# Three plain feed-forward chunks instead of four, later down units, other places for the down inputs

## The chip, the cores and the metric

The kernel runs on one core of a Trainium2 chip. The metric is device time in microseconds (us) for one launch, the median of several runs. The core has a matmul engine (TensorE, here PE), a vector engine (VectorE, DVE), an activation engine (ScalarE, ACT), a general engine (GpSimd, POOL) and a queue that issues most transfers (SyncE, SP). They run side by side and wait for each other through semaphores.

## The reference

Two layers of an encoder, 512 tokens of 1024 channels, float32. Each has three branches (two attentions and a pooling) that are merged, and then a gated feed-forward part with 2 x 2816 inner channels:

```
hf = rms_norm(x, ffn_norm_g[l])
u = depthwise_conv(hf @ ffn_w_up[l], ffn_conv_w[l], ffn_conv_b[l])   # width 3 over tokens
u_gate, u_val = u[..., :D_FF], u[..., D_FF:]
x = x + (jax.nn.silu(u_gate) * u_val) @ ffn_w_down[l]
```

Only the schedule of this last part changes.

## The kernel before, in words

**Numbers.** Every float32 operand is split into a high and a low half, and each product is three matmuls: high by high, low by high, high by low (`mm3`). Activations lie with channels on the 128 partitions and the 512 tokens along the row.

**Chunks.** The 2816 inner channels are 22 chunks of 128. A chunk has a gate part (part 0) and a value part (part 1). It can be made in two ways.

- A *plain* chunk (`plain`) multiplies each part with all eight blocks of 128 input channels: 8 x 3 matmuls of 128x512 per part, 48 in all, into one PSUM bank per part.
- A chunk of *products* (`product`) takes gate and value rows, odd and even input blocks, and first and second half of the tokens as a 2x2 by 2x2 block product and makes it with seven products instead of eight. They are named 11, 12, 1, 22, 2, 4, 3 (`FORMS`, in this order). Each has four steps of three matmuls of 128x256, so 12, and the chunk 84. Products 11, 12 and 4 read the normalized input (tiles HH, HL); 1, 2, 22 and 3 read sums of its blocks (tiles `tf`), which `build_forms` makes on DVE and ACT once per layer, while the plain chunks run on PE.

**What else a chunk needs.** The weights come from HBM by SP into `raw` tiles. A plain piece is split by ACT (`wh`) and by DVE, POOL or an accumulating transfer (`wl`). For a chunk of products four blocks of 128x512 arrive. Blocks 11, 12, 22 are split into `fh` and `fl`, where the low half is finished by a transfer that POOL issues (`by_transfer`); for products 1, 2, 4, 3 DVE sums blocks, ACT takes the high half and DVE the low one (`w_form`). Weight units are made up to six units ahead of their use (`wnext`, LAF). Behind the products DVE adds the banks to saved pieces (`sx`, by ACT), scales by the norm, adds the two neighbours of the convolution, multiplies gate by value and makes the low half; ACT does the middle tap, the SiLU and the high half.

**Down units.** A down unit (`down`) is three matmuls of 128x512: one chunk of the group before, into one block m of 128 output channels. The units of a group g go over its 8 blocks m, and over its chunks i inside; after the last i DVE adds the bank (`ps_mi`, `ps_S` in turn) to the residual XM. So no unit of a group can come before the group's chunk that it reads is finished and split.

**The order.** The chunks form groups (`SIZES`). `_ffn` writes PE's order out: all plain chunks of group 0, then for each chunk of products the seven products, and after products 22, 2, 4 and 3 (`SPOTS`, four *places* per chunk) some down units of the group before, dealt evenly over the group's places. Two chunks' worth (`KEEP` 2 output blocks) of the last-but-one group's units and all of the last group's come behind the last product. `_stream` derives the order of the weight loads from the same list. The orders of DVE, ACT, POOL and SP come out of a model of the engines' times inside the kernel (`Clock`), which decides only order, while the program is written.

**Where the halves wait.** A chunk's high and low half wait for the down units of the next group. The first ones of a group take fixed places (six pairs in four wide tiles `act`, `PLACE`), the others two slots each (`ah`, `al`) of a pool of 47 slots of 128x512 that all temporary tiles share (`keep_act`).

In the last layer the last block m is made in two token halves (`half`, `out_half`), so that its first half can be stored earlier; of each unit but the last three the second half follows at once.

Of the kernel before, what the change touches and what calls it, by code (L numbers as in the profile page):

```python
# [21 lines left out]
KC = D // P  # L22
# [4 lines left out]
FC = D_FF // P  # L27
# [14 lines left out]
PRE_A = 16  # L42
PRE_B = 8
LA, LAP, LAF = 3, 4, 6
SIZES = (4, 5, 5, 5, 3)
PLACE = ((0, 1, 2, 3), (4, 5), (0, 1, 2, 3), (4, 5), (0, 1, 2))
KEEP = 2
FORMS = ("11", "12", "1", "22", "2", "4", "3")
SPOTS = ("22", "2", "4", "3")
END = object()  # L50
RSQRT_BITS = 1597463007.0
SLACK = 35
# [57 lines left out]
def _groups():  # L110
    e = np.cumsum(SIZES)
    return [(int(b - n), int(b)) for n, b in zip(SIZES, e)]


def _ffn():

    toks, late = [], []
    for g, (c0, c1) in enumerate(_groups()):  # L120
        dealt = len(late) - (KEEP * SIZES[g - 1] if g == len(SIZES) - 1 else 0)
        for n, c in enumerate(range(c0, c1)):
            if g == 0:
                toks += [("u", c, 0), ("u", c, 1)]
                continue
            now = late[:dealt * (n + 1) // (c1 - c0) - dealt * n // (c1 - c0)]
            late = late[len(now):]
            for f in FORMS:
                toks.append(("f", c, f))
                if f in SPOTS:  # L130
                    k = SPOTS.index(f)
                    toks += now[len(now) * k // len(SPOTS):len(now) * (k + 1) // len(SPOTS)]
        late += [("d", g, m, i) for m in range(KC) for i in range(c1 - c0)]
    return toks + late


def _layer_units():

    r = _widths()
    for tok in _ffn():  # L140
        if tok[0] == "u":
            r += [("u", T), ("p", T), ("next",)]
        elif tok[0] == "f":
            r.append(tok)
        elif (tok[2] * SIZES[tok[1]] + tok[3]) % 4 == 0:
            r.append(("u" if tok[1] < len(SIZES) - 1 else "p", T))
    return r


def _stream():  # L150
# [4 lines left out]
    for kind, *u in _layer_units() * L:  # L155
        if kind == "next":
            plain = (plain + 1) % (2 * SIZES[0])
            if plain >= 2 * SIZES[0] - 8 or not plain:
# [179 lines left out]
def trunk(ctx: ExitStack, tc: tile.TileContext, x, w, prm, gb, cst, out):  # L338
# [344 lines left out]
    def layer(l, sq, xsrc):  # L683
# [331 lines left out]
        def gates(br, okey, odst, mode):  # L1015
# [48 lines left out]
            for k, m in _order(br):  # L1064
# [5 lines left out]
                while more:  # L1070
                    n = tick - first
                    if extra and (tick % 2 == 0 if when == "q" else k == "g" and n in ((2, 6) if when == "n" else (3,))):
                        if next(extra, END) is END:
                            extra = None
                        yield
                    tick += 1
                    more = next(work, END) is not END
                    yield
# [570 lines left out]
        def keep_act(c):  # L1649
            g = next(i for i, (c0, c1) in enumerate(groups) if c0 <= c < c1)  # L1650
            i = c - groups[g][0]
            if i < len(PLACE[g]):
                n = 2 * PLACE[g][i]
                return places[n], places[n + 1]
# [156 lines left out]
        for kind, *tok in _ffn():  # L1811
            {"u": plain, "f": product, "d": down}[kind](*tok)
# [64 lines left out]
def _pack_weights(i):  # L1877
    res = []
    for l in range(L):
# [34 lines left out]
        for kind, *tok in _ffn():  # L1914
            if kind == "u":
                c, part = tok
                o = D_FF * part + c * P
                res += _cut(_blocks(up[:, o:o + P], KC))
            elif kind == "f" and tok[1] == FORMS[0]:
                for o in (0, D_FF):  # L1920
                    b = _blocks(up[:, o + tok[0] * P:o + tok[0] * P + P], KC).reshape(P, KC // 2, 2, P)
                    res += [b[:, :, k].reshape(P, T) for k in range(2)]
            elif kind == "d":
                g, m, k = tok
                c0, c1 = _groups()[g]
                if (m * (c1 - c0) + k) % 4 == 0:
                    at = [divmod(m * (c1 - c0) + k + n, c1 - c0) for n in range(4)]
                    res.append(np.concatenate([dn[(c0 + k_) * P:(c0 + k_ + 1) * P, m_ * P:m_ * P + P]
                                               for m_, k_ in at], axis=1))
# [82 lines left out]
```

## Time and profile before

| | |
|---|---|
| median of 3 runs | 1545.17 us (1543.88 to 1545.56) |
| the profiled execution's own time | 1543.25 us |
| its span, first to last instruction | 1541.4 us |
| feed-forward stage of layer 0 | 425.27 to 771.49 us |
| plain chunks of layer 0 | 425.27 to 469.04 us |
| chunks of products of layer 0 | 469.04 to 748.37 us |
| feed-forward stage of layer 1 | from 1191.7 us to the end |

The span is what the trace shows; the execution's own time has 1.85 us more around it. Times in rows of the trace are microseconds from the start of the span. A row of a group or instruction names the line, the engine, the operation and output<-inputs without buffer numbers. A matmul's row shows longer than the distance to the next one, since matmuls overlap; PE's pace is read from start to start, or from a long stretch divided by its count. Lines are those of the kernel before; the changed kernel's are 14 higher behind the edit.

### The profile page before, as it was taken

The numbers are of one execution on the slowest core, as the hardware profiler recorded it, in microseconds if no ns is written. First come the engines' busy times: TensorE is split into PE (matmuls) and PEld (weight loads), VectorE is DVE, ScalarE is ACT, GpSimd is POOL, SyncE is SP. The second block draws the span as 40 slices with busy tenths as digits, with TensorE's granted clock in tenths as the row PEclk, the third lists the DMA queues.
The fourth block names the chain that finished last, engine by engine and source line by source line (L and its number), as shares of the span: only waits on it lengthen the run. The fifth ranks groups of instructions, "written<-read, shape, count | busy, mean of one in ns | idle before, by whom it ended". The sixth has DMA issues, their size and how long they took to land.

```text
span 1541.4 us, 24574 instructions
## 1 busy us (share of the span) xinstructions
PE 1535.9 (100%) x8337; PEld 1343.0 (87%) x8337; DVE 1157.5 (75%) x1955; ACT 1079.5 (70%) x2018; POOL 765.6 (50%) x829
## 2 busy tenths in 40 slices
PE   9999999999999999999999999999999999999999
PEld 8888888888889999999898888888888899999997
DVE  6767886776688888888746588768666888888885
ACT  6567875877677877777554587758766677777772
POOL 3874886753452323232488648776535522222222
PEclk9999999999999999999999999999999999999999
DMA  7432354658978878877554423547599788787863
GB/s 239 113 117 83 88 125 141 161 130 205 235 170 195 181 184 187 190 175 160 139 148 126 118 74 88 125 144 174 117 217 217 193 183 191 178 188 190 179 140 109
DMA packets 140381, 243.36 MB, mean 158 GB/s; under 512 B 31072, under 2 KB 53600, under 8 KB 140256
## 3 DMA queue, kind: packets, MB, share of 16 engines
q1 hardware_dynamic: 91872, 162.93, 34.2%
q0 software_dynamic: 43488, 78.66, 29.7%
q8 instruction: 65, 1.06, 0.3%
q10 hardware_dynamic: 4896, 0.21, 0.2%
q14 instruction: 60, 0.49, 0.1%
HBM read 149.41 MB, written 13.63 MB: 106 GB/s over the span
## 4 chain that ended last, share of the span: by engine, by line
PE 95%; DMA 2%; POOL 1%; issue 1%; DVE 1%; ACT 0%; SPq 0%; POOLq 0%; ACTq 0%; DVEq 0%
PE ps_acc L526 42%; PE ps_AV L526 17%; PE ps_ST L526 16%; PE ps_S L526 10%; PE ps_mi L526 9%; DMA XM<-x 1%; DMA qb<-nm 1%; DMA raw<-w 0%; POOL win L306 0%; DMA tf<-dl 0%; POOL tabg L306 0%; POOL tabm L306 0%; POOL fac L306 0%; POOL wl L306 0%; POOL ssc L306 0%
## 5 line engine op out<-in xcount | busy, mean ns | idle before, releaser
L438 POOL DMA_DIRECT2D wl<-raw x194 | 174.9, 908 | 407.2 <-ACT wl L299 183.8
L299 ACT ACTIVATE wh<-raw 128x512 fp32r<-128x512 f32 (+2 forms) x449 | 265.0, 605 | 61.4 <-DMA raw<-w 17.6
L306 POOL TENSOR_TENSOR wl<-raw,wh 128x512 fp32r<-128x512 f32 (+2 forms) x164 | 204.9, 1258 | 147.1 <-ACT wh L299 141.5
L438 POOL DMA_DIRECT2D fl<-raw x108 | 94.2, 872 | 167.5 <-ACT fl L299 67.3
L526 PE MATMUL ps_acc<-HH,wh 128*128 128x512 f32 x400 | 156.7, 392 | 0.0
L526 PE MATMUL ps_acc<-HH,wl 128*128 128x512 f32 x400 | 156.4, 391 | 0.0
L526 PE MATMUL ps_acc<-HL,wh 128*128 128x512 f32 x400 | 156.4, 391 | 0.0
L310 DVE SCALAR_TENSOR_TENSOR a<-u,prm,a 128x511 f32<-128x511 f32 x176 | 134.4, 766 | 19.0 <-ACT a L299 18.4
L299 ACT ACTIVATE wl<-wh 128x512 fp32r<-128x512 f32 (+1 forms) x194 | 121.9, 628 | 6.2
L314 DVE TENSOR_REDUCE nm<-ps_S 128x1 fp32r<-128x512 f32 x128 | 87.7, 686 | 44.2 <-PE ps_S L526 43.6
L299 ACT ACTIVATE a<-u,prm 128x512 f32<-128x512 f32 x88 | 71.2, 812 | 56.2 <-DVE u L306 56.0
L526 PE MATMUL ps_acc<-tf,wh 128*128 128x256 f32 x576 | 106.2, 282 | 0.0
L526 PEld LDWEIGHTS ps_acc<-tf,wh 128*128 128x128 f32 x576 | 94.3, 191 | 6.0
L526 PEld LDWEIGHTS ps_acc<-HH,wl 128*128 128x128 f32 x400 | 75.1, 188 | 16.3
L526 PEld LDWEIGHTS ps_acc<-HL,wh 128*128 128x128 f32 x400 | 75.2, 188 | 15.4
L526 PEld LDWEIGHTS ps_acc<-HH,wh 128*128 128x128 f32 x400 | 75.3, 188 | 15.1 <-issue 0.4
L526 PE MATMUL ps_acc<-tf,wl 128*128 128x256 f32 x288 | 81.5, 283 | 0.0
L306 DVE TENSOR_TENSOR wl<-raw,wh 128x512 fp32r<-128x512 f32 (+1 forms) x92 | 64.3, 700 | 18.6 <-ACT wh L299 18.2
L526 PE MATMUL ps_AV<-HH,wl 128*128 128x256 f32 (+1 forms) x240 | 78.2, 326 | 0.0
L526 PE MATMUL ps_AV<-HH,wh 128*128 128x256 f32 (+1 forms) x240 | 78.1, 326 | 0.0
L526 PE MATMUL ps_AV<-HL,wh 128*128 128x256 f32 (+1 forms) x240 | 78.1, 326 | 0.0
L306 DVE TENSOR_TENSOR pl<-ps_ST,ph 128x512 fp32r<-128x512 f32 x86 | 58.3, 682 | 17.8 <-ACT ph L299 14.3
(427 smaller groups left out, 5028.2 us busy)
## 6 DMA issues: line engine op xcount, KB each, us to landing
raw<-w SPq DMA_DIRECT2D x153, 512.0 KB, 4.0
wl<-raw POOLq DMA_DIRECT2D x190, 256.0 KB, 4.2
raw<-w SPq DMA_DIRECT2D x151, 256.0 KB, 3.8
fl<-raw POOLq DMA_DIRECT2D x108, 256.0 KB, 5.0
raw<-w SPq DMA_DIRECT2D x13, 384.0 KB, 3.1
XM<-x SPq DMA_DIRECT2D x16, 256.0 KB, 4.4
dtq<-tr SPq DMA_DIRECT2D x16, 192.0 KB, 1.9
dtk<-tr SPq DMA_DIRECT2D x16, 192.0 KB, 3.0
```

The source lines that it names most:

```text
L299: return self.eng.activation(out, in_, func, **k)
L306: return self.eng.tensor_tensor(out, *a)
L310: return self.eng.scalar_tensor_tensor(out, *a)
L314: return self.eng.tensor_reduce(out, in_, *a, **k)
L438: nc.gpsimd.dma_start(f(lo), r, accum_op=ALU.add)
L526: PE.matmul(o, lhsT=lhsT, rhs=rhs, start=start, stop=stop, skip_group_check=again)
```

## The change

Group 0 has three plain chunks instead of four and the last group four chunks of products instead of three, so that 19 chunks of a layer are made by products instead of 18. The places are counted through from the first chunk of products. A new table `SKIP` lets the down units of groups 1, 2 and 3 (dealt while groups 2, 3 and 4 are made) begin one place later; the first place of such a group still takes units of the group before. The fixed places are given out as 0 to 2 and 3 to 5 by turns.

```
-SIZES = (4, 5, 5, 5, 3)
-PLACE = ((0, 1, 2, 3), (4, 5), (0, 1, 2, 3), (4, 5), (0, 1, 2))
+SIZES = (3, 5, 5, 5, 4)
+PLACE = ((0, 1, 2), (3, 4, 5), (0, 1, 2), (3, 4, 5), (0, 1, 2))
 KEEP = 2
 FORMS = ("11", "12", "1", "22", "2", "4", "3")
 SPOTS = ("22", "2", "4", "3")
+SKIP = (0, 0, 1, 1, 1)
...
+def _dealt():
+
+    starts = [len(SPOTS) * (c0 - SIZES[0]) + n for (c0, _), n in zip(_groups(), SKIP)]
+    at = [0] * (len(SPOTS) * (FC - SIZES[0]))
+    for g in range(1, len(SIZES)):
+        a, n = starts[g], starts[g + 1 if g + 1 < len(SIZES) else g] - starts[g]
+        units = KC * SIZES[g - 1]
+        if not n:
+            n = len(at) - a
+            units -= KEEP * SIZES[g - 1]
+        for s in range(n):
+            at[a + s] = units * (s + 1) // n - units * s // n
+    return at
...
-    toks, late = [], []
+    toks, late, dealt = [], [], iter(_dealt())
     for g, (c0, c1) in enumerate(_groups()):
-        dealt = len(late) - (KEEP * SIZES[g - 1] if g == len(SIZES) - 1 else 0)
         for n, c in enumerate(range(c0, c1)):
             if g == 0:
                 toks += [("u", c, 0), ("u", c, 1)]
                 continue
-            now = late[:dealt * (n + 1) // (c1 - c0) - dealt * n // (c1 - c0)]
-            late = late[len(now):]
             for f in FORMS:
                 toks.append(("f", c, f))
                 if f in SPOTS:
-                    k = SPOTS.index(f)
-                    toks += now[len(now) * k // len(SPOTS):len(now) * (k + 1) // len(SPOTS)]
+                    k = next(dealt)
+                    toks += late[:k]
+                    late = late[k:]
         late += [("d", g, m, i) for m in range(KC) for i in range(c1 - c0)]
     return toks + late
```

The new deal puts 24 units on 21 places (1 each, 2 at three of them), then 2 on each of the other 55. Before it was 32 on 20 places, 40 on 20, 40 on 20 and 30 on 12.

PE behind the third plain chunk of layer 0, before: the last matmuls of its value part (bank ps_AV) and the first of the fourth plain chunk (`wh`, `wl` are split weights).

```order
L526 MATMUL ps_AV_4988<-HH,wh_4942 128x512
L526 MATMUL ps_AV_4988<-HL,wh_4942 128x512
L526 MATMUL ps_AV_4988<-HH,wl_4943 128x512
L526 MATMUL ps_acc_5047<-HH,wh_4946 128x512
L526 MATMUL ps_acc_5047<-HL,wh_4946 128x512
L526 MATMUL ps_acc_5047<-HH,wl_4947 128x512
```

The same place after: product 11 of the first chunk of products follows (`fh`, `fl` are the halves of block 11).

```order
L540 MATMUL ps_AV_4998<-HH,wh_4899 128x512
L540 MATMUL ps_AV_4998<-HL,wh_4899 128x512
L540 MATMUL ps_AV_4998<-HH,wl_4900 128x512
L540 MATMUL ps_acc_5052<-HH,fh_4903 128x256
L540 MATMUL ps_acc_5052<-HL,fh_4903 128x256
L540 MATMUL ps_acc_5052<-HH,fl_4904 128x256
```

The two parts of the fourth plain chunk (48 matmuls of 128x512) are gone from here, and the products stand in their place.

PE at the first place of group 4 in layer 0, before: the end of product 22 (bank ps_ST), the first two down units of group 3 (bank ps_mi, halves in the fixed places `act`) and product 2.

```order
L526 MATMUL ps_ST_8144<-tf_4766,fh_8010 128x256 x2
L526 MATMUL ps_ST_8144<-tf_4766,fl_8011 128x256
L526 MATMUL ps_mi_8172<-act_4721,wh_8028 128x512
L526 MATMUL ps_mi_8172<-act_4722,wh_8028 128x512
L526 MATMUL ps_mi_8172<-act_4721,wl_8029 128x512
L526 MATMUL ps_mi_8172<-act_4722,wh_8028 128x512 x2
L526 MATMUL ps_mi_8172<-act_4722,wl_8029 128x512
L526 MATMUL ps_acc_8081<-tf_4458,wh_8042 128x256 x2
```

After: the units in that place are the last two of group 2 (bank ps_S, halves in slots `ah`, `al`).

```order
L540 MATMUL ps_ST_8016<-tf_4766,fh_7876 128x256 x2
L540 MATMUL ps_ST_8016<-tf_4766,fl_7877 128x256
L540 MATMUL ps_S_7899<-ah_6738,wh_7789 128x512
L540 MATMUL ps_S_7899<-al_6739,wh_7789 128x512
L540 MATMUL ps_S_7899<-ah_6738,wl_7790 128x512
L540 MATMUL ps_S_7899<-ah_6936,wh_7789 128x512
L540 MATMUL ps_S_7899<-al_6937,wh_7789 128x512
L540 MATMUL ps_S_7899<-ah_6936,wl_7790 128x512
L540 MATMUL ps_acc_7948<-tf_4458,wh_7905 128x256 x2
```

Group 3's first unit has moved behind product 2.

DVE while the plain chunks run, before: the last sums for `tf`, the work on plain parts (u, a, act), and the first weight sum for the products (raw by raw).

```order
L306 TENSOR_TENSOR tf_4767<-tt_4763,tf_4767 128x256
L306 TENSOR_TENSOR u_4939<-ps_acc_4887,rbc_4823 128x512
L310 SCALAR_TENSOR_TENSOR a_4886<-u_4885,prm_91,a_4886 128x511
L306 TENSOR_TENSOR a_4831<-a_4831,a_4774 128x512
L310 SCALAR_TENSOR_TENSOR a_4940<-u_4939,prm_91,a_4940 128x511 x2
L306 TENSOR_TENSOR act_4719<-a_4831,act_4719 128x512
L306 TENSOR_TENSOR a_4940<-a_4940,a_4886 128x512
L306 TENSOR_TENSOR u_4986<-ps_ST_4941,rbc_4823 128x512
L306 TENSOR_TENSOR act_4720<-a_4940,act_4719 128x512
L310 SCALAR_TENSOR_TENSOR a_4987<-u_4986,prm_91,a_4987 128x511 x2
L306 TENSOR_TENSOR raw_4650<-raw_4650,raw_4660 128x512
```

After:

```order
L324 SCALAR_TENSOR_TENSOR a_4888<-u_4887,prm_91,a_4888 128x511
L320 TENSOR_TENSOR raw_4650<-raw_4650,raw_4660 128x512
L320 TENSOR_TENSOR u_4950<-ps_acc_4889,rbc_4823 128x512
L320 TENSOR_TENSOR tf_4767<-tt_4763,tf_4767 128x256
L324 SCALAR_TENSOR_TENSOR a_4888<-u_4887,prm_91,a_4888 128x511
L320 TENSOR_TENSOR a_4831<-a_4831,a_4774 128x512
L320 TENSOR_TENSOR wl_4954<-raw_4650,wh_4953 128x512
```

The weight sum has moved ahead of the last `tf` row, some ten rows earlier, between the plain parts' work. The orders of the attention part of layer 1 are the same on every engine.

## The prediction

> **What bounds the kernel now.** I began with the page: engine times, then the chain that ended last.
>
> ```profile
> span 1541.4 us, 24574 instructions
> PE 1535.9 (100%) x8337; PEld 1343.0 (87%) x8337; DVE 1157.5 (75%) x1955; ACT 1079.5 (70%) x2018; POOL 765.6 (50%) x829
> ...
> PE 95%; DMA 2%; POOL 1%; issue 1%; DVE 1%; ACT 0%; SPq 0%; POOLq 0%; ACTq 0%; DVEq 0%
> ```
>
> The chain is TensorE (PE) for 95%. A busy PE may hide short waits, so the second view is the list of what PE waited for over the whole span (total, times, longest).
>
> ```profile
> PE ps_mi L1833 <- DVE keep L334: 1.1, 1, 1.1
> PE ps_ST L526 <- DMA qb<-nm: 0.6, 1, 0.6
> PE ps_acc L526 <- POOL wl L306: 0.6, 1, 0.6
> ```
>
> All of it is 2.3 us, none of it in the feed-forward stage. The third view cuts that stage of layer 0 at its groups: the plain chunks, groups 1, 2, 3 and 4 (chunks of seven products, with down units between them), and the down units left at the end. Each row starts with its length; busy times of PE, PEld, DVE, ACT, POOL follow.
>
> ```profile
> 425.27:469.04 43.77, 43.77 (x196) 36.26 (x194) 37.49 (x58) 29.64 (x51) 23.29 (x20) 1.00 0.75 185
> 469.04:541.49 72.45, 72.45 (x517) 68.32 (x516) 62.75 (x107) 57.09 (x107) 19.92 (x23) 1.00 0.81 179
> 541.49:619.49 78.00, 78.00 (x541) 72.86 (x540) 63.96 (x109) 59.02 (x110) 21.73 (x25) 1.00 0.82 186
> 619.49:697.49 78.00, 78.00 (x541) 72.86 (x540) 63.96 (x109) 59.02 (x110) 21.65 (x25) 1.00 0.80 185
> 697.49:748.37 50.88, 50.88 (x343) 47.10 (x342) 37.72 (x64) 35.67 (x67) 15.01 (x17) 1.00 0.68 143
> 748.37:771.49 23.12, 23.12 (x103) 19.14 (x102) 18.07 (x23) 12.78 (x22) 14.39 (x11) 1.00 0.44 141
> ```
>
> The fourth is the chain by pieces (start, length, matmuls): two plain pieces, four products, down units singly and in pairs.
>
> ```profile
> 458.32 5.44 PE ps_acc L526 x24
> 463.76 5.44 PE ps_ST L526 x24
> 469.20 1.43 PE ps_acc L526 x12
> 470.63 1.44 PE ps_ST L526 x12
> 472.07 1.44 PE ps_AV L526 x12
> 473.51 1.44 PE ps_ST L526 x12
> 474.95 0.70 PE ps_mi L526 x3
> 475.65 1.43 PE ps_acc L526 x12
> 477.08 1.39 PE ps_mi L526 x6
> ```
>
> A 128x512 matmul takes 5.44 / 24 = 0.227 us, a 128x256 one 1.44 / 12 = 0.120. Group 2 has five chunks of 84 small matmuls and 40 units of 3 large ones: 420 x 0.120 + 120 x 0.227 = 77.6, against 78.00 measured. The other 0.4 us is 0.02 for each of 20 changes between the sizes. PE therefore runs at its own pace here: the stage is the sum of its matmuls, and a change is worth what it takes off that sum, less any wait it creates.
>
> **One chunk fewer is plain.** In each layer 48 large matmuls go, two pieces of 5.44 = 10.88 us. In their place comes a chunk of seven products. Its cost is read from group 2, where 40 units of 3 x 0.227 = 0.68 us are 27.2: (78.00 - 27.2) / 5 = 10.16 us with the changes of size. Group 1 gives (72.45 - 32 x 0.68) / 5 = 10.14; without changes of size it is 84 x 0.120 = 10.08. I take 10.16, since the new chunk has units at all four of its places: **-0.72 us a layer**, with -0.74 and -0.80 as the other ends. It all counts, since PE is the path on both sides.
>
> The Trainium skill has another price: in "TensorE: Matmul & The Clock Gate", section "Back-to-back issue gap", an isolated warm matmul takes N / 2.4 + 2.5 ns, so 109 ns and 216 ns for the two sizes. By that the chunk would save 48 x 0.216 - 84 x 0.109 = 1.2 us a layer, an estimate from that page. The rows above disagree, with 120 and 227 ns: 11 ns above the Trainium skill's figure for either size, so the version with more matmuls pays more often.
>
> **Down units are dealt anew.** The groups' units were 32, 40, 40, 40, 24 and are 24, 40, 40, 40, 32: 176 in both. Moving a unit costs PE nothing. Group 1 now takes 5 x 10.16 + 22 x 0.68 = 65.8 us instead of 72.45, group 4 four chunks at 78.00 / 5 = 15.60 instead of three in 50.88, and the end 42 units instead of 34: 23.12 + 8 x 0.68 = 28.6.
>
> **Beginning one place later.** This takes away no PE wait, for there is none. It lengthens a lead. A short lead stands at the start of group 4: DVE's last half of group 3, and its first use.
>
> ```profile
> 706.00 0.69 DVE L306 TENSOR_TENSOR al<-a,ah 128x512 fp32r<-128x512 f32 x1 [1.33 <-ACT ah L299]
> ...
> 707.68 0.39 PE L526 MATMUL ps_mi<-al,wh 128*128 128x512 f32 x1
> ```
>
> The lead is 707.68 - 706.69 = 0.99 us. In the new order a place comes first, a product and two units or 2.8 us. At the end of the stage the last chunk's use comes one unit (0.68 us) later too.
>
> **Where the halves are kept.** Three chunks of each group now lie in the fixed places, two (one in group 4) in slots. No instruction is added. A place of group 2 was last read at group 2's first place for units, two products or more before it is written. Cost: nothing, and up to a few tenths should slots free later; a gain is excluded, since nobody waits for them.
>
> **The closing.** The last channel block of layer 1 runs in halves: 24 matmuls of 128x256 instead of 18. Beside the same units whole that is 24 x 0.120 - 12 x 0.227 = 0.16 instead of 0.12: +0.04 us.
>
> **Other engines.** The extra chunk brings four weight sums, four low halves, four additions and scalings to DVE, and three transfers issued by POOL. On SP's queue its weights are four loads of 256 KB where the plain chunk had two of 512, the same bytes, and the first product chunk's loads keep their rank. All of it hides beneath PE if DVE keeps up (below).
>
> **The sum** is 2 x -0.72 + 0.04 = **-1.40 us**: span 1541.4 to 1540.0, the profiled execution 1543.25 to 1541.85. The median of the runs lies 1.9 above that execution, so 1545.17 - 1.4 = **1543.8 us**.
>
> **The rivals.** *DVE becomes the bound of group 1 (slower).* Group 1 leaves 65.8 us for five chunks and eight residual additions. DVE was busy 63.96 us with just these in group 2, or 97% of that. Moreover it waits for others than PE (total over the stage, times, longest):
>
> ```profile
> DVE a L310 <- ACT a L299: 9.2, 23, 1.6
> DVE act L306 <- ACT act L299: 8.5, 8, 4.0
> DVE u L306 <- ACT wl L299: 5.4, 4, 1.9
> DVE wl L306 <- ACT wh L299: 5.0, 9, 2.3
> DVE al L306 <- ACT ah L299: 3.7, 5, 1.3
> ```
>
> That is 31.8 us over 22 chunks, 7.2 for five. If every wait stayed, DVE would need 63.96 + 7.2 = 71.2, 5.4 too many: 2 x 5.4 - 1.4 = +9.4, or 1554.6 us. It decides from 2.3 us of waiting a layer. Against it:
>
> ```profile
> 508.43 0.42 DVE L306 TENSOR_TENSOR u<-ps_AV,sx 128x256 f32<-128x256 f32 x1 [1.15 <-PE ps_AV L526]
> 508.89 0.69 DVE L306 TENSOR_TENSOR u<-u,rbc 128x512 f32<-128x512 f32 x1
> 509.50 0.68 DVE L306 TENSOR_TENSOR s<-raw,raw 128x512 f32<-128x512 f32 x1
> 510.10 0.68 DVE L306 TENSOR_TENSOR XM<-ps_S,XM 128x512 f32<-128x512 f32 x1
> 510.70 0.74 DVE L310 SCALAR_TENSOR_TENSOR a<-u,prm,a 128x511 f32<-128x511 f32 x1
> 511.36 0.42 DVE L306 TENSOR_TENSOR u<-ps_acc,sx 128x256 f32<-128x256 f32 x1
> ```
>
> Queued instructions overlap their ends: a start follows after 0.60 us, not 0.69, after a convolution's 0.66, after a half-width addition from PSUM about 0.34. A chunk (12 full-width, 4 convolutions, 4 half-width, 1.6 residual) then needs 12 x 0.60 + 4 x 0.66 + 4 x 0.34 + 1.6 x 0.60 = 12.2 us; five need 61, or 93% of 65.8. Also DVE waits here for PE (1.15 us), so it is ahead, and weight halves are made well before use:
>
> ```profile
> 501.59 0.68 DVE L306 TENSOR_TENSOR wl<-raw,wh 128x512 fp32r<-128x512 f32 x1
> ...
> 506.96 0.28 PE L526 MATMUL ps_AV<-HH,wl 128*128 128x256 f32 x1
> ```
>
> That lead of 4.7 us would have to be used up first. Chance 7%.
>
> *The products start before their inputs are there (slower).* They now begin 10.88 us sooner after the stage's start, at about 458.2.
>
> ```profile
> 418.35 3.08 SPq L407 DMA_DIRECT2D raw<-w  x4
> ...
> 448.60 0.41 DVE L306 TENSOR_TENSOR tf<-tt,tf 128x256 fp32r<-128x256 f32 x1
> ...
> fl<-raw POOLq DMA_DIRECT2D x108, 256.0 KB, 5.0
> ```
>
> The first chunk's weights are asked for by 421.4, and the last moving operand is ready at 449.0, 12 us before the first product that reads one. One late transfer of 5.0 us a layer would give 2 x 5.0 - 1.4 = +8.6: 1553.8 us. Chance 4%.
>
> *Short waits eat the gain.* Denser products shorten leads; waits of 0.6 to 2.2 us a layer end between -0.2 and +3.0 us, 1545.0 to 1548.2. Chance 11%.
>
> *Matmuls pack closer in the new mix.* The rows' 227 and 120 ns differ by 107 ns for 256 columns, which leaves 13 ns on each matmul whatever its size. Were that gone, the chunk would save 48 x 0.214 - 84 x 0.107 = 1.3 us a layer: -2.5 with the closing, 1542.7 us. Against it, every row of the stage carries the 13 ns. Chance 2%. (The rule of the Trainium skill named above goes this way, with 1.2 us a layer.)
>
> *Faster by more than 3 us.* The 2.3 us that PE waited lie outside the stage and the order there does not move. Only scatter of the runs could show it. Chance 4%.
>
> **How the numbers follow.** My forecast has the other 72%. About 0.2% (3.1 us) is what a measurement of this kernel can tell from no change, so the forecast, the short waits and the closer packing are all "same": 72 + 11 + 2 = 85%. Slower is 7 + 4 = 11%, faster 4%. The forecast's own bounds are 2 x 0.72 to 2 x 0.80, 1543.6 to 1543.8; the runs of before lie 1.3 below and 0.4 above their median, and as much again is allowed downward for the closer packing: 1541.9. Upward the range takes in most of the short waits: 1547.3. Outside lie the two slow rivals and part of the 4%.
>
> **What the profile after would show.** Plain chunks end near 458.2 in layer 0, with three chunks of 10.9; group 1 lasts about 65.7 us, every later chunk 15.60, the end 28.6; PE's waits stay near 2.3 us in all. In group 1 DVE's busy share rises from 87% to 93% or more with no PE wait for it. The forecast is wrong if PE rows waiting for DVE, ACT or a transfer appear between 458 and 771, if group 1 is longer than 66.5, or if the rest of the kernel differs by over a microsecond.

## The result, and the profile after

| | before | after |
|---|---|---|
| median, same chip (21 runs each) | 1544.12 us (1542.90 to 1545.91) | 1541.84 us (1540.95 to 1544.44) |
| the profiled execution's own time | 1543.25 us | 1542.16 us |
| its span | 1541.4 us | 1540.0 us |

The ratio is 0.9986, with a 95% interval of 0.9980 to 0.9992: a small gain, inside the 0.2% that were called "same". The interval, from 1.2 to 3.1 us, holds the 1.40 us of the sum at its near end. The median itself, 1541.84, lies 0.06 us below the lower end of the range; why is told further down.

First the page after: span, PE and the other engines, and the engines' shares of the chain that ended last.

```profile
span 1540.0 us, 24712 instructions
PE 1534.9 (100%) x8412; PEld 1344.5 (87%) x8412; DVE 1164.9 (76%) x1978; ACT 1087.8 (71%) x2030; POOL 763.3 (50%) x828
...
PE 96%; ACT 1%; issue 1%; DMA 1%; DVE 0%; POOL 0%; SPq 0%; ACTq 0%; POOLq 0%; DVEq 0%
```

The list of what PE waited for over the whole span (total, times, longest) is as short as before, 1.7 us for 2.3.

```profile
PE ps_mi L1847 <- DVE keep L348: 1.1, 1, 1.1
PE ps_acc L540 <- POOL wl L320: 0.4, 1, 0.4
PE ps_ST L540 <- DMA fl<-raw: 0.2, 1, 0.2
```

The feed-forward stage of layer 0, cut at its groups (length; then busy times of PE, PEld, DVE, ACT, POOL): plain chunks, groups 1 to 4, and the units left at the end.

```profile
425.10:457.99 32.89, 32.89 (x148) 27.25 (x146) 30.72 (x47) 23.33 (x41) 18.98 (x16) 1.00 0.79 199
457.99:523.82 65.83, 65.78 (x488) 62.59 (x486) 60.88 (x106) 53.82 (x102) 17.32 (x20) 1.00 0.84 195
523.82:601.82 78.00, 78.00 (x542) 72.86 (x541) 66.01 (x114) 60.96 (x113) 21.71 (x25) 1.00 0.83 183
601.82:679.82 78.00, 78.00 (x542) 72.86 (x541) 63.88 (x109) 59.83 (x111) 21.64 (x25) 1.00 0.83 186
679.82:742.22 62.40, 62.40 (x434) 58.29 (x433) 49.20 (x82) 45.66 (x85) 17.81 (x21) 1.00 0.67 143
742.22:770.77 28.55, 28.55 (x127) 23.65 (x126) 20.14 (x25) 15.17 (x26) 19.75 (x16) 1.00 0.48 157
```

The landmarks foreseen are there. The plain chunks end 32.89 us after the start, which is 3 x 10.88 and 0.25. Group 1 lasts 65.83 us, the four chunks of group 4 take 62.40, or 15.60 each, and the end 28.55. DVE is busy for 60.88 of group 1's 65.83 us, 92%, and PE does not wait for it.

The stages of both layers, from the first matmul of one to the first of the next, in the profiled runs:

| us | attention 0 | feed-forward 0 | attention 1 | feed-forward 1 | after the last matmul |
|---|---|---|---|---|---|
| before | 425.27 | 346.22 | 420.23 | 346.42 | 3.29 |
| after | 425.10 | 345.67 | 419.56 | 346.18 | 3.47 |
| after, second profile | 425.88 | 345.85 | 419.82 | 345.52 | 3.48 |

The last matmul is counted with 0.12 us. The feed-forward stages give 0.55 + 0.24 = 0.79 us in one profile and 0.37 + 0.90 = 1.27 in the other, for 1.40 in the sum. So the span's 1540.0 us, which is what the sum gave, is in part luck: 0.79 us came from the feed-forward stages, 0.84 from attention, where nothing had changed, and 0.18 were lost at the end. What is missing in the stages are short waits that fall elsewhere from run to run. Two of the first profile show in the chain. In layer 0 product 3 waits for ACT (start, length, what):

```profile
467.96 0.61 ACT wh L313
468.57 0.28 ACT sx L313
468.85 0.04 issue
468.90 1.69 PE ps_acc L540 x12
```

Product 3 adds into the bank of product 2, which ACT must have copied (`sx`) first. In ACT's order the copy stood behind the splitting of a weight (`wh`). The twelve matmuls take 1.69 us for the usual 1.44. Group 1 now has places with one unit where it had two, so less PE work lies between products 2 and 3. In the second profile this place has no such wait; there one of 0.4 us falls at 515.9 us. In layer 1 a weight's accumulating transfer landed late:

```profile
1244.88 6.66 DMA fl<-raw
1251.54 0.04 issue
1251.58 1.46 PE ps_ST L540 x10
```

It took 6.66 us, where the median of such transfers in the kernel before was 5.0. PE's next start came 0.34 us later than usual.

### The profile page after: what moved, and what is told of

Same layout as the page of the kernel before. It is cut to its first block, busy times and chain, and to the rows that moved or that the text cites. A ratio compares the mean times of both kernels' runs of the same rounds, so it can differ in the third digit from the quotient of the medians.

```text
span 1540.0 us, 24712 instructions
## 1 busy us (share of the span) xinstructions
PE 1534.9 (100%) x8412; PEld 1344.5 (87%) x8412; DVE 1164.9 (76%) x1978; ACT 1087.8 (71%) x2030; POOL 763.3 (50%) x828
## 4 chain that ended last, share of the span: by engine, by line
PE 96%; ACT 1%; issue 1%; DMA 1%; DVE 0%; POOL 0%; SPq 0%; ACTq 0%; POOLq 0%; DVEq 0%
PE ps_acc L540 42%; PE ps_AV L540 18%; PE ps_ST L540 16%; PE ps_S L540 10%; PE ps_mi L540 9%; DMA fl<-raw 0%; ACT a L313 0%; DMA XM<-x 0%; ACT wh L313 0%; POOL fac L320 0%; ACT fh L313 0%; DMA raw<-w 0%; ACT fl L313 0%; ACT L313 0%; DVE fac L320 0%
## 5 line engine op out<-in xcount | busy, mean ns | idle before, releaser
L452 POOL DMA_DIRECT2D wl<-raw x186 | 168.5, 913 | 432.3 <-ACT wl L313 197.4
L313 ACT ACTIVATE wh<-raw 128x512 fp32r<-128x512 f32 (+3 forms) x445 | 265.2, 607 | 89.0 <-DMA raw<-w 18.2
L320 POOL TENSOR_TENSOR wl<-raw,wh 128x512 fp32r<-128x512 f32 (+3 forms) x165 | 206.0, 1257 | 133.7 <-ACT wh L313 123.3
L452 POOL DMA_DIRECT2D fl<-raw x114 | 100.1, 878 | 155.3 <-ACT fl L313 53.0
L540 PE MATMUL ps_acc<-HH,wh 128*128 128x512 f32 x384 | 150.5, 392 | 0.0
L540 PE MATMUL ps_acc<-HH,wl 128*128 128x512 f32 x384 | 150.2, 391 | 0.0
L540 PE MATMUL ps_acc<-HL,wh 128*128 128x512 f32 x384 | 150.1, 391 | 0.0
L313 ACT ACTIVATE wl<-wh 128x512 fp32r<-128x512 f32 (+1 forms) x186 | 116.8, 628 | 5.9
L540 PE MATMUL ps_acc<-tf,wh 128*128 128x256 f32 x608 | 112.2, 282 | 0.0
L313 ACT ACTIVATE a<-u,prm 128x512 f32<-128x512 f32 x88 | 71.2, 812 | 54.3 <-DVE u L320 53.8
L313 ACT ACTIVATE fl<-fh 128x512 fp32r<-128x512 f32 x114 | 72.2, 633 | 3.6
```

The costliest lines, as they stand in the source:

```text
L313: return self.eng.activation(out, in_, func, **k)
L320: return self.eng.tensor_tensor(out, *a)
L452: nc.gpsimd.dma_start(f(lo), r, accum_op=ALU.add)
L540: PE.matmul(o, lhsT=lhsT, rhs=rhs, start=start, stop=stop, skip_group_check=again)
```

## The experiments

All runs are compared with runs of the kernel before on the same chip. "After" is the changed kernel.

**After, once more.** No edit.

> The changed kernel as it is, for more timings and a second profile. The sum of the matmuls gives -1.4 us against before; the first profile of it shows -0.79 in the two feed-forward stages (two short waits of 0.3 and 0.6 us ate the rest) and -0.8 in the attention stages, whose orders are unchanged. If the latter is scatter, the feed-forward stages of layer 0 and 1 come out again near 345.7 and 346.2 us (346.22 and 346.42 before), and the attention stages anywhere within about 1 us of 425.3 and 420.2. If the change does help the attention stages, they come out near 425.1 and 419.6 again.

Measured: 1541.59 us against 1543.62, ratio 0.9985 (0.9975 to 0.9994). The result repeats. Its stages stand in the table above.

**After, without the later start.**

```
-SKIP = (0, 0, 1, 1, 1)
+SKIP = (0, 0, 0, 0, 0)
```

> The changed kernel with every group's down units beginning at its first place (all numbers of SKIP 0). Theory that PE's time is the sum of its matmuls: as the changed kernel within 0.5 us, no PE wait for a half of a group's last chunk, since with two units a place its last chunk is read at the third place, 2 us later than before the change. Rival, that the later start is what makes the change pay: PE waits at the starts of groups 2, 3 and 4 in both layers, 2 us or more slower than the changed kernel.

Measured: 1542.35 us, ratio 0.9990 (0.9981 to 0.9998). That is 0.8 us above after on the same chip, more than the 0.5 us allowed for, but the intervals overlap, so it is not to be told from after. The stages are 346.17 and 345.52 us, after's 345.67 and 346.18. PE does not wait at any start of a group, though the halves in slots come only 2 to 3 us ahead of their use there. Its one wait in the stage of layer 0, 0.4 us, is again for ACT's `sx`, at the end of group 1.

**After, with the places of before.**

```
-PLACE = ((0, 1, 2), (3, 4, 5), (0, 1, 2), (3, 4, 5), (0, 1, 2))
+PLACE = ((0, 1, 2, 3), (4, 5), (0, 1, 2, 3), (4, 5), (0, 1, 2))
```

> The changed kernel with the fixed places given out as before the change (0 to 3 and 4, 5 by turns); no instruction more or less. Theory: the places cost and bring nothing, so as the changed kernel within 0.5 us, and the same feed-forward stages. Rival, that slots free later and loads wait for them: SP's loads of weights start later, PE waits for weights, 1 us or more slower.

Measured: 1542.00 us, ratio 0.9989 (0.9980 to 0.9998), stages 345.60 and 345.69. The places bring and cost nothing that can be seen.

**Before, with the later start alone.**

```
-SIZES = (3, 5, 5, 5, 4)
-PLACE = ((0, 1, 2), (3, 4, 5), (0, 1, 2), (3, 4, 5), (0, 1, 2))
+SIZES = (4, 5, 5, 5, 3)
+PLACE = ((0, 1, 2, 3), (4, 5), (0, 1, 2, 3), (4, 5), (0, 1, 2))
```

> Sizes and places of the kernel before, with the down units of groups 2, 3 and 4 dealt from one place later. The theory (the gain is the plain chunk that became a chunk of products; dealing the units out otherwise costs and brings nothing) expects the same matmuls as before and feed-forward stages of 346.2 and 346.4 us, each within 0.5 us, and a time within 1 us of the kernel before on the same chip. The rival (the later start itself pays) expects a time lower by 1 us or more, with the stages shorter by 0.4 us or more each.

Measured: 1543.36 us against 1544.05, ratio 0.9993 (0.9984 to 1.0002), stages 346.19 and 346.78. The new dealing is worth nothing that can be seen; the rival asked for stages 0.4 us shorter. So the gain is put down to the sizes, the one part of the change that is left. This run also shows what attention scatters by. Its order there is that of before and after, and PE's list has

```profile
PE ps_ST L540 <- DMA qb<-nm: 1.2, 1, 1.2
```

a wait of 1.2 us that was 0.6 in the profile of before and is missing in that of after.

**Two plain chunks.**

```
-SIZES = (3, 5, 5, 5, 4)
-PLACE = ((0, 1, 2), (3, 4, 5), (0, 1, 2), (3, 4, 5), (0, 1, 2))
+SIZES = (2, 5, 5, 5, 5)
+PLACE = ((0, 1), (3, 4, 5), (0, 1, 2), (3, 4, 5), (0, 1, 2))
```

> One step further: two plain chunks, then groups of 5 5 5 5. Theory, PE's sum alone: another 0.72 us less per layer, 1.4 us faster than the changed kernel, about 2.8 faster than before. Rival, DVE or the transfers become the bound of the first group: it has 16 units on 20 places, so PE needs 5 x 10.16 + 16 x 0.68 = 61.7 us for five chunks where DVE needs 61 by starts and 64 by busy time, beside what the plain chunks leave it; waits of 3 us or more a layer, and the kernel no faster than the changed one or slower. Rival, inputs not there in time: the first product that reads a sum starts at about 450.2, when the last sum is 1.2 us old, so a wait at the first chunk.

Measured: 1549.38 us, ratio 1.0034 (1.0022 to 1.0045), stages 349.94 and 348.84. PE's list:

```profile
PE ps_mi L540 <- DVE act L320: 2.7, 2, 1.4
PE ps_mi L540 <- ACT act L313: 2.0, 2, 1.0
PE ps_acc L540 <- ACT sx L313: 1.1, 3, 0.4
```

The first two rows are the first down units of group 1, once in each layer. The chain in layer 0 ends in the half that such a unit reads:

```profile
456.39 0.69 DVE a L320
457.08 0.61 DVE act L320
457.70 0.04 issue
457.74 1.22 PE ps_mi L540 x2
```

The plain chunks' halves are made once the norm of the tokens is there, some 16 us into the stage. With two plain chunks the units come before them. In layer 0 the wait cost more than its length. The starts of the unit's first two matmuls came 2.8 us later than usual, and from 457.53 us on the clock was granted at 0.50 for 3.41 us. The next twelve small matmuls, most of them in this stretch, took 2.37 us for 1.44:

```profile
457.53:460.94 3.41, 3.20 (x13) 3.02 (x14) 2.65 (x5) 1.70 (x4) 0.87 (x1) 0.50 1.02 207
```

In layer 1 the same waits left the clock at 1.00, and that stage is 1.1 us shorter.

**Two plain chunks, their units four places later.** The run before with

```
-SKIP = (0, 0, 1, 1, 1)
+SKIP = (0, 4, 1, 1, 1)
```

> Sizes 2 5 5 5 5 as in the run with two plain chunks, but the down units of group 0 begin four places later in group 1. The theory (that run lost its time to first down units which came before the two plain chunks' halves were through ScalarE and VectorE) expects the waits of about 3 us at the start of group 1 to go in both layers, so at least 6 us less than that run's 1549.4 us. If nothing else then ends late, the second plain chunk turned into products brings another 0.7 us a layer, and the time is about 1540 to 1542 us. The rival (with two plain chunks VectorE or ScalarE sets the pace of group 1, whatever the dealing) expects waits of 3 us or more to stay later in group 1 and a time of 1546 us or more.

Measured: 1544.45 us against 1544.05, ratio 1.0006 (0.9997 to 1.0015), stages 346.73 and 346.86. The waits for the halves are gone, so that cause is shown; by the ratios 4.3 us came back, where at least 6 were said. But the 1540 to 1542 us did not come, nor did the rival's waits later in group 1. Another wait took the place, 1.74 us beyond the usual distance of two matmuls in each layer, at product 3 of the first chunk of products:

```profile
457.73 0.36 ACT sx L313
458.09 0.52 ACT wh L313
458.61 0.52 ACT act L313
459.13 0.28 ACT sx L313
459.46 3.14 PE ps_acc L540 x24
```

ACT is still busy with the plain chunks (`act`) and with weights when the products need their copies. Without the wait the stage of layer 0 would take 346.73 - 1.74 = 344.99 us, which is after's 345.67 less the 0.7 of one more chunk turned over; layer 1 would take 345.12, for 346.18 and 345.52 in the two profiles of after. So the price of a chunk agrees here too, to some tenths. That three plain chunks are where ACT's backlog from the start of the stage is just covered is what this suggests; no run moved ACT's work alone.

**VectorE loaded on purpose.** Two kernels ask what DVE had to spare: after, with two or with five more instructions at the end of each product chunk's chain. They read constants and write a column that nobody reads.

```
+    spare = cp.tile([P, 1], F32, tag="spare", name="spare")
...
+        extra = [lambda: V.tensor_reduce(spare, C[:, :T], AX.X, ALU.add)] * 2
...
-                chain(..., *scale(v), *convolve(c, 1, v))
+                chain(..., *scale(v), *convolve(c, 1, v), *extra)
```

> The changed kernel with two more VectorE instructions (each reads 128x512 constants and writes a spare column, about 0.6 us) at the end of the chain of each of the twenty chunks of products of a layer. No other engine reads them. Reading A (VectorE's need in group 1 is the sum of its instructions from start to start, 61 us, so this makes 67 us against TensorE's 65.8, and the lead of about 2.6 us over TensorE covers the difference) expects at most 0.5 us a layer, 1 us in all. Reading B (its real need is nearer 65 us with the gaps that its waits leave, so this makes 71 us) expects 2 to 5 us a layer, with TensorE waiting for VectorE's outputs late in group 1, and the later groups unchanged at 78.0 us.

> The same with five more instructions a chunk, 3 us. Reading A expects group 1 to need 76 us on VectorE against 65.8, so some 7 to 10 us more in each layer, all of it in group 1, and groups 2 and 3 still at 78.0 us: 14 to 20 us in all. Reading B expects group 1 at about 81 us and groups 2 and 3 also longer, by 2 to 3 us each: over 35 us in all. A theory in which VectorE has slack enough everywhere expects less than 2 us.

(A layer has nineteen such chunks, not twenty; the figures for group 1 go by its five.) Measured: 1548.82 us, ratio 1.0032 (1.0021 to 1.0043), and 1569.20 us, ratio 1.0164 (1.0150 to 1.0178). Read alone, the first would favour reading B: some 7 us above after, whose ratio is 0.9986. But attention, where nothing was added, had become 3.3 and 4.2 us longer, and the plain chunks took 33.83 us for 32.89. So the control was needed:

**The tile without the instructions.** Only the line `spare = ...` is added, as an unused tile.

> The changed kernel with one unused constant tile of 32 bytes a partition, which moves the weight halves and all temporary tiles by 32 bytes against the normalized input HH and HL; no instruction is added. In the two runs with extra VectorE instructions, which also had that tile, a 128x512 matmul that reads HH or HL with weight halves took 0.234 us for 0.227 and a 128x256 one 0.117 for 0.120. The theory (the distance of the two operands' addresses, 32 bytes off a multiple of 64, does that) expects both here: attention stages of about 428.4 and 423.6 us, plain chunks 33.8 us a layer, the products about 1.2 us a layer shorter, and 1546 to 1549 us; the two extra instructions a chunk then cost less than 0.5 us a layer. The rival (the extra instructions did it) expects the changed kernel's time, within 1 us.

Measured: 1548.53 us, ratio 1.0034 (1.0022 to 1.0047); attention 429.17 and 423.46, plain chunks 33.83, stages 345.31 and 345.46. The theory holds: the tile alone does it, by moving the tiles behind it by 32 bytes. The same pieces of the chain after, and with the unused tile:

```profile
425.26 5.44 PE ps_acc L540 x24
```

```profile
429.33 5.60 PE ps_acc L540 x24
```

24 matmuls of 128x512 take 5.60 us for 5.44.

Against this control the load on DVE can be read. Group 1 and groups 2 and 3 of the control:

```profile
463.00:528.27 65.27, 65.27 (x488) 62.42 (x487) 60.10 (x105) 53.08 (x101) 17.31 (x20) 1.00 0.83 193
528.27:606.00 77.73, 77.73 (x542) 72.57 (x541) 66.23 (x114) 61.21 (x113) 21.70 (x25) 1.00 0.82 185
606.00:683.73 77.73, 77.73 (x542) 72.58 (x540) 63.83 (x109) 59.78 (x111) 21.64 (x25) 1.00 0.83 187
```

With two more instructions a chunk, groups 1 and 2:

```profile
462.21:527.48 65.27, 65.27 (x488) 62.42 (x486) 61.32 (x107) 53.12 (x101) 17.54 (x21) 1.00 0.77 175
527.48:605.21 77.73, 77.73 (x542) 72.58 (x540) 72.72 (x127) 60.66 (x112) 21.57 (x25) 1.00 0.87 193
```

Not a hundredth is lost in either; the stages are 345.46 and 345.54 us, 0.15 and 0.08 above the control. With five, groups 1 to 3:

```profile
462.26:528.51 66.25, 65.52 (x487) 62.47 (x486) 62.73 (x110) 52.80 (x100) 17.59 (x21) 1.00 0.77 176
528.51:615.05 86.54, 80.51 (x542) 74.42 (x540) 82.72 (x144) 60.60 (x112) 21.52 (x25) 0.96 0.73 168
615.05:692.78 77.73, 77.73 (x541) 72.58 (x540) 76.65 (x134) 60.80 (x112) 22.10 (x26) 1.00 0.83 187
```

The stages are 10.8 and 10.2 us longer than the control's. In layer 0 0.98 us are lost in group 1, 8.81 early in group 2 and 0.98 in the units at the end. In group 2 PE asks for the halves that the late chain makes:

```profile
PE ps_mi L540 <- ACT ah L313: 9.4, 2, 4.7
PE ps_mi L540 <- DVE al L320: 2.7, 2, 1.3
PE ps_acc L540 <- DVE wl L320: 1.5, 2, 0.7
```

Group 3 loses nothing, with DVE busy for 76.65 of 77.73 us. Reading A holds in the main: DVE needs about 61 us for group 1, and with 5 x 5 x 0.60 = 15 more 76 against 65.3, 10.7 too many; 9.8 were paid in groups 1 and 2. It is a debt of group 1 that shows at the start of group 2, where reading A had put it in group 1. The near match of the two numbers is partly chance. PE stood still for 6.8 of the 9.8 us (the lengths less PE's busy times); the other 3.0 are a slower pace, because behind the long wait the clock was granted at 0.50:

```profile
547.16:553.99 6.83, 5.14 (x16) 4.15 (x17) 6.80 (x13) 1.66 (x3) 0.00 (x0) 0.50 0.44 154
```

A 128x512 matmul took 0.43 us there, and layer 1 has the same. Reading B would have made group 3 longer as well.

**Addresses, on purpose.** In the control the 128x256 matmuls that read the normalized input had become quicker: the median distance from start to start was 117 ns for 120, against 233 for 227 with 128x512. Three kernels try to keep the one and not the other. The first begins the halves of the forms 1, 2, 4 and 3 later by 32 bytes:

```
-NSLOT = 47
+NSLOT = 46
+OFF = 8
...
-        return (hlp.tile([P, T], F32R, tag="wh", name=f"wh{j}"), hlp.tile([P, T], F32R, tag="wl", name=f"wl{j}"))
+        o = OFF * (units[j][0] not in "pu")
+        return tuple(hlp.tile([P, T + OFF + 8], F32R, tag=n, name=f"{n}{j}")[:, o:o + T] for n in ("wh", "wl"))
```

> The changed kernel with the halves of the block forms for products 1, 2, 4 and 3 begun 32 bytes later in their tiles (made 64 bytes wider, for which one of the 47 slots is given up). 912 of a layer's 1596 matmuls of 128x256 then read operands 32 bytes off a multiple of 64 apart, and no matmul of 128x512 does. At 1.4 to 3 ns each the theory (their distance sets the pace) expects 1.3 to 2.7 us less in each feed-forward stage, so 1536 to 1539 us. The rival (the pace came from elsewhere, or the missing slot costs more) expects 1541 us or more.

The second also moves the temporary tiles, with a table `SIDE` by weight unit, and an unused 32-byte tile between the pools:

```
-        o = OFF * (units[j][0] not in "pu")
+        o = OFF * SIDE[j]
```

> As the run before, with the temporary tiles moved by 32 bytes too, and every weight half placed by what it is multiplied with: a 128x512 matmul a multiple of 64 bytes from its other operand, 1368 of a layer's 1596 matmuls of 128x256 32 bytes off it. The theory expects 1.9 to 4.1 us less in each feed-forward stage than in the changed kernel, and attention stages as there: 1533.5 to 1538 us. The rival expects 1541 us or more.

The third is the first with wider tiles:

```
-        ... hlp.tile([P, T + OFF + 8], ...
+        ... hlp.tile([P, T + 4 * OFF], ...
```

> As the run with the block forms' halves begun 32 bytes later, but with tiles 128 bytes wider instead of 64, so that all tiles again begin at multiples of 128 bytes. In that run the 128x256 matmuls took 0.118 us for 0.120, as expected, but every 128x512 one 0.232 for 0.227, with half of the tiles at odd multiples of 64. The theory (both operands at multiples of 128 bytes give 0.227, and 32 bytes apart 0.118 for the small ones) expects attention stages of about 425.5 and 420 us again, and feed-forward stages 1 to 2 us shorter than the changed kernel's 345.5 to 346.2: 1538 to 1540 us. The rival (what the 512-column matmuls lost has to do with the offset or the missing slot, not with 64 bytes) expects them at 0.232 again and 1552 us or more.

Measured: 1553.72 (ratio 1.0066, 1.0053 to 1.0080), 1552.81 (1.0060, 1.0046 to 1.0074) and 1553.40 us (1.0063, 1.0049 to 1.0076). All three missed. The small matmuls that were moved did get quicker, 118 ns for 120. But the 128x512 ones that had taken 227 ns, attention's too, took 231 or 232, at tiles of 64 as of 128 bytes more. Six of attention's, after and in the third kernel:

```profile
46.67 1.36 PE ps_AV L540 x6
```

```profile
47.27 1.39 PE ps_AV L542 x6
```

A multiple of 64 or of 128 bytes between two operands is therefore not what gives 227. The three kernels share the later halves, the wider tiles and the missing slot (`NSLOT` 46), and none of these was tried alone. None of these versions beats after.

## Why the prediction was right, point by point

**TensorE's own pace.** Right. The chain stayed PE's, and the prices taken from before give the groups of after to 0.1 us. Two errors cancel in group 1, though: its price was 0.3 us too high, by the next point, and it holds a wait of 0.3 us.

**One chunk fewer is plain.** Right in kind; the size was read too small, and waits hid it. The prediction took a down unit at 3 x 0.227 = 0.68 us and put the 0.4 us that its sum for group 2 lacked down to changes between the sizes. Its own rows show two units in 1.39 us, so one takes 0.695. In group 2 the distance is 233 ns behind a unit's first two matmuls and 228 or 227 behind the third, while the changes of size cost nothing (120 ns behind a small matmul, 227 behind a large one). With 0.695 both groups give the same chunk: (78.00 - 27.8) / 5 = 10.04 and (72.45 - 22.24) / 5 = 10.04 us. So the exchange is worth 10.88 - 10.04 = 0.84 us a layer instead of 0.72, and the sum is -1.64 instead of -1.40. Measured were -0.55 and -0.24 in one profile and -0.37 and -0.90 in the other. The run with four plain chunks and the new dealing had none of it. The run with two plain chunks and late units, its one wait taken off, has it again.

**Dealing anew, later start, places.** Right as far as can be seen: each was set at nothing, and each undone or done alone gave nothing beyond the scatter; the intervals leave some 1 us either way. The short lead that the prediction quoted was real but nobody waited for it.

**The closing.** +0.04 us was said. From the last matmul to the end of the span it is 0.18 us more in addition, in every run with a group 4 of four chunks, and some 0.3 more in the two with five (3.60 for 3.29). The last store starts as early after its addition as before, and the span ends later behind it. Why was not tried.

**DVE as the bound of group 1.** Rightly set low, for the right reason. Start-to-start distances gave 61 us against 65.8, the sum of busy time and waits 71.2. The loaded runs bear out the first: two more instructions a chunk cost 0.15 and 0.08 us a layer, where 71 us would have cost 2 to 5.

**Products before their inputs.** It did not happen with three plain chunks. With two PE did wait at the start of the products, but for other things than the prediction named: not the weights or the moving operands came late, but the plain chunks' halves, and then ACT's copies behind a backlog. The prediction did not price these two margins.

**Short waits.** This rival set in, below its price: of the 1.64 us that the exchange is worth, 0.85 were eaten in one profile and 0.37 in the other, where it began at 1.2 for both layers. The waits seen in the starts make up for it to 0.1 us in layer 0: 0.3 us at product 3 in the first profile and 0.5 in the second, with what PE loses just behind them. A PE wait for ACT between 458 and 771 us was named as a sign that the forecast is wrong. By that sign the claim of no new wait failed in layer 0, by these tenths.

**Closer packing.** Its premise, 13 ns on each matmul whatever its size, stood in every row of the stage and yet was no constant of the engine, as the unused tile showed. There the distances are 117 and 233 ns, which leaves next to nothing of the 13. In after itself nothing packed closer.

**The number.** 1543.8 us was said, 1541.84 came. Half of that is the level. "The median of the runs lies 1.9 above that execution" rested on three runs; over 21 runs the median of before is 1544.12, so 0.87 above it. That is 1.05 us of the 1.96. The other 0.9 is the difference of the medians, -2.28 for -1.40, which the interval allows. Two terms behind it were put at nothing. The time around the span was taken over from before, 1.85 us; after's profiled execution has 2.16, and all its 21 runs 2.1 to 2.2, for reasons that no run shows. So the span itself fell by some 2.6 us in the medians. And attention was expected to stay: it was 0.84 us shorter in one profile of after and 0.20 us longer in the other, with the same order. Over six profiles (before, after twice, the runs without the later start, with the old places and with the later start alone) its two stages add up to 844.7 to 846.2 us, and single waits for one transfer (`qb<-nm`) there range from none listed to 1.2 us. The feed-forward stages give at most 1.64 us, so the traces do not show a cause for all of it. Whether -2.28 is more than scatter stays open. The low end of the range, 1541.9, is not plainly worked out: 1543.6 less 1.3 and less 1.3 again is 1541.0.

## What to carry to other kernels

Where one engine runs back to back, price an exchange of instructions by start-to-start distances from a long stretch; here that gave a stage of 346 us to half a microsecond. Read each kind of instruction by itself: what a sum lacks may lie in another kind than the one suspected, and then the price of an exchange is off although the total fits. Measure another engine's slack the same way, not by its busy share, which was 99% of group 3 in one run without costing anything, and test it by adding instructions that nobody needs; what it lacks may be paid a group later, and here a long wait cost more than its length. When a test adds a tile, run the tile alone too, since it moves the others.

## What the runs showed of the hardware

TensorE's pace depended on where its operands lie. With an unused 32-byte tile ahead of the weight halves and temporary tiles, matmuls that read HH or HL with weight halves took 233 ns at 128x512 for 227 and 117 ns at 128x256 for 120 (medians from start to start), at the same clock of 1.00; those whose two operands both moved, such as the merged input with its weights, kept 227. So the small ones gain and the large ones lose. With tiles widened by 64 or 128 bytes, one slot fewer and some halves begun later, those of the merged input took 231 or 232 ns as well. The matmuls of the down units had a median of 231 ns in before and after alike, and 231 or 232 in all these kernels. Which bits of the addresses decide, and through what, was not settled. It cost some 7 to 12 us (ratios of 1.0034 to 1.0066 to the kernel before, for after's 0.9986), several times the change studied here.

The Trainium skill's rule for an isolated matmul in "TensorE: Matmul & The Clock Gate", section "Back-to-back issue gap", N / 2.4 + 2.5 ns, has no term for this. At 117 and 233 ns the trace lies 8 and 17 ns above its 109 and 216, at 120 and 227 ns 11 and 11, so the excess is no constant for each matmul.

A long wait of PE was followed by a lower clock. With five more VectorE instructions a chunk, PE's start came 4.86 us later than usual, and the clock was then granted at 0.50 for 6.83 us, in both layers. With two plain chunks two waits of 1.15 and 1.62 us were followed by 3.41 us at 0.50 in layer 0, and the same two by none in layer 1. The single wait of 1.74 us with the late units left the clock at 1.00. What decides was not tried.
